# Mixer output to first gate products of a decoder layer: an order by hand, last steps by tiles, and 114-row transfers split into 112 and 2

## The chip, the cores and the metric

The kernel runs on one core of a Trainium2 chip. The metric is the device time of one execution in microseconds (us). The profile is one execution of the same program, recorded by the hardware profiler. Engines are called PE (matmul; PEld is its weight load), DVE (vector), ACT (activation), POOL (GpSimd) and SP (the engine that issues most transfers). A name such as L1017 is a line of the kernel.

## The reference

One decoder layer on 1024 tokens with 16 learned meta tokens ahead of them, width 1024, float32 throughout. A mixer gives `z`; the change lies between `z` and the gate matmul of the feed-forward part. Cut to that:

```python
def rmsnorm(x, gain):
    y = x * lax.rsqrt(jnp.mean(x * x, axis=-1, keepdims=True) + EPS)
    return y * gain
...
        h = h + rmsnorm(z @ w_out[l], mix_norm_post[l])
        u = rmsnorm(h, ffn_norm_pre[l])
        gt = causal_dwconv(u @ ffn_w_gate[l], ffn_conv_w[l], ffn_conv_b[l])
        y = (jax.nn.gelu(gt, approximate=True) * (u @ ffn_w_up[l])) @ ffn_w_down[l]
        h = h + rmsnorm(y, ffn_norm_post[l])
```

## The kernel before

**Numbers.** Every float32 operand is cut into a high part (a cast by ACT) and a low part (operand minus high part, by DVE or POOL). A product is three matmuls, high x high, high x low, low x high (`mm3`, L158 to L162). A weight block `wraw` is loaded by SP, ACT casts it to `whi` (L136, in the gate part L209), and POOL or DVE subtracts to get `wlo` (L137, L210). There are three buffers of `whi` and `wlo`, and the loader keeps three blocks ahead.

**The output projection.** The tokens are cut into three chunks (`c`) of 342, and each chunk into three tiles of 114 rows (RT). For a chunk, `mix_mm` runs over eight k steps; a step multiplies one 128-row block of `z` with one block of `w_out`, for three tiles and two halves of 512 columns: 18 matmuls, named `pm`. Each tile's sum lies in a pair of PSUM banks. There are four pairs; three of them hold the chunk, and the fourth is for transposes (`pt`). The blocks of `z` come from `split_z` (casts and subtractions `zc`, L938 and L939). The last two blocks of weights of chunk 2 have their low part from DVE, all others from POOL.

**Behind a chunk.** For each tile `mix_out` squares the sums on ACT (L1085, result to `ssq2`) and multiplies them by the gain on DVE (L1086, to `m`), each in two halves of 512 columns; after that the pair of banks is empty. `vec` adds the two sums of squares (L1093), takes the reciprocal root, adds the residual row (L1095), stores the new `h` to DRAM as `hscr` (L1096) and normalises again for the feed-forward part: square on ACT (L340), and a multiply by root and gain on DVE in two halves (L345), to `un`. `feat` transposes `un` with eight PE transposes (L1017) and cuts the result into quarters: `v1` (b11, b21) for the first half of the tokens, and for the second half t1 to t4 and b22, which are sums and differences with the first half (L1020 to L1042). The pieces of a chunk are run between the k steps of the next one, by the list that `reorder` gives; those of chunk 2 between the first gate products.

**The gate products.** The gate and up matmuls use one level of Strassen's scheme (`Strassen`): each unit of 128 columns pairs has seven products P1 to P7 (line names `P`, L262 to L265), and each product has 24 matmuls of 258 or 256 columns or 12 of 512. P1 and P2 need only the first half of the tokens (b11, b21). So the first four units run P1 and P2 early: P1(0), P1(1), P2(0), P2(1), P1(2), P1(3), P2(2), P2(3), in the code from `ffn.begin()` on (L1264). Then comes `finish`, which begins with the P6 of unit 0 and reads t2. `ahead(n)` casts the weights of the next n products; `load_first` loads the weights of the early units, `load_unit` those of a whole unit, with sums on POOL (L235 to L238). The result of P1 is copied to SBUF by ACT, the result of P2 is added to it by DVE (`g`, L1191).

**What sets the order.** A scheduler at build time puts the instructions of each engine in an order of its own, from the program, except in `finish`, where POOL's order is that of the code. Each engine then runs its row in order, and an instruction that waits holds all those behind it on that engine.

Of the kernel before, what the change touches and what calls it, by code (L numbers as in the profile page):

```python
# [14 lines left out]
P = 128  # L15
D = 1024
# [40 lines left out]
def trunk_kernel(ctx: ExitStack, tc: tile.TileContext, x, meta_tokens, mix_norm_pre,  # L57
# [122 lines left out]
    class Strassen:  # L180
# [7 lines left out]
        def __init__(self, units, run, early, quarters, span, put, whole):  # L188
# [8 lines left out]
            self.got, self.at = [], 0  # L197
# [50 lines left out]
        def product(self, u, p):  # L248
# [8 lines left out]
            for k in range(4):  # L257
# [6 lines left out]
                for c, o, w in cuts:  # L264
                    pe.matmul(x[:, o : o + w], wlo[:, k, :], xh[:, c : c + w], start=False, stop=(k == 3))  # L265
            self.ahead(4)
            return x[:, o0 : o0 + n]
# [14 lines left out]
        def first(self, u):  # L282
# [3 lines left out]
            return (lambda: act.copy(self.p1s[u], self.product(u, "P1")),  # L286
                    lambda: self.put(u, 0, 0, self.p1s[u], self.product(u, "P2")))
# [711 lines left out]

    def load_res(t0):  # L1000
        row = slot(D, name="row2")
        if t0 == 0:
            nc.sync.dma_start(row[:HALO], meta_tokens[T0:NM, :])
            nc.sync.dma_start(row[HALO:RT], x[0, 0 : RT - HALO, :])
        else:
            nc.sync.dma_start(row[:RT], x[0, t0 - HALO : t0 - HALO + RT, :])
# [48 lines left out]
    def mix_mm(c, between, zs):  # L1055
        rows.update({c * CW + i * RT: load_res(c * CW + i * RT) for i in range(3)})
        banks = [pair_banks("pm") for _ in range(3)]
        znext = []
        for k in range(KD):
            whi, wlo = wo.next()  # L1060
            if k == KD - 1 and c < 2:
                znext = [split_z(c + 1, k_) for k_ in range(ZA)]
            zh, zl = zs[k]
            for i in range(3):
                t = slice(i * RT, (i + 1) * RT)
                for j in range(2):
                    n = slice(j * 512, (j + 1) * 512)
                    mm3(banks[i][j][:RT], (zh[:, t], zl[:, t]), (whi[:, 0, n], wlo[:, 0, n]), k == 0, k == KD - 1)
            wo.ahead()
            if k + ZA < KD:  # L1070
                zs.append(split_z(c, k + ZA))
            if between:
                for f in between.pop(0):
                    f()
        return banks, znext

    def mix_out(c, banks, g2, g3):
        todo = []
        for i in range(3):
            m1 = slot(D, name="m1")  # L1080
            ssq = small([P, 2], "ssq2", "mq", 6)
            for j in range(2):
                n = slice(j * 512, (j + 1) * 512)
                junk = t_tmp(512, "junk")
# [344 lines left out]
```

## Time and profile before

| | us |
|---|---|
| median of 3 runs | 1434.69 |
| lowest and highest | 1431.66, 1434.87 |
| the profiled execution | 1431.93 |
| its span, first to last instruction | 1430.1 |

The mean granted clock of PE in the profiled execution was 0.979 of full speed. The difference of 1.8 us between the execution's time and the span lies around the recorded instructions. How long a group of instructions takes is read from its mean duration; whether it matters is read from who waits for it. A pause of PE and the stretch at a lower granted clock that follows it are read together.

### The profile page before, as it was taken

The numbers are of one execution on the slowest core, as the hardware profiler recorded it, in microseconds if no ns is written. First come the engines' busy times: TensorE is split into PE (matmuls) and PEld (weight loads), VectorE is DVE, ScalarE is ACT, GpSimd is POOL, SyncE is SP. The second block draws the span as 40 slices with busy tenths as digits, with TensorE's granted clock in tenths as the row PEclk, the third lists the DMA queues.
The fourth block names the chain that finished last, engine by engine and source line by source line (L and its number), as shares of the span: only waits on it lengthen the run. The fifth ranks groups of instructions, "written<-read, shape, count | busy, mean of one in ns | idle before, by whom it ended". The sixth has DMA issues, their size and how long they took to land. (4 is left out here: it accounts for less than half of the span.)

```text
span 1430.1 us, 21631 instructions
## 1 busy us (share of the span) xinstructions
PE 1364.1 (95%) x8405; PEld 1233.2 (86%) x8405; DVE 976.1 (68%) x1406; ACT 570.1 (40%) x981; POOL 570.3 (40%) x400
## 2 busy tenths in 40 slices
PE   8989999999999999998968999999999999999976
PEld 6789999999999899976658888888899998888765
DVE  6784545489876754625678888888888775445476
ACT  6443333366654452244464322322222233333353
POOL 4255421237354410253348565544556642001051
PEclk9999999999999999999988999999999999999998
DMA  6034333321110033644542577666677798565546
GB/s 240 36 97 141 126 111 104 97 60 45 33 47 5 23 133 103 218 139 153 166 126 80 142 232 206 186 174 158 162 166 165 169 259 232 194 194 180 191 158 218
DMA packets 129562, 202.65 MB, mean 142 GB/s; under 512 B 7739, under 2 KB 75935, under 8 KB 129460
## 3 DMA queue, kind: packets, MB, share of 16 engines
q1 hardware_dynamic: 118548, 181.08, 37.9%
q0 software_dynamic: 10912, 20.19, 9.4%
q8 instruction: 66, 1.08, 0.3%
q14 instruction: 36, 0.29, 0.1%
HBM read 152.45 MB, written 71.85 MB: 157 GB/s over the span
## 5 line engine op out<-in xcount | busy, mean ns | idle before, releaser
L137 POOL TENSOR_TENSOR wlo<-wraw,whi 128x1024 fp32r<-128x1024 f32 (+2 forms) x37 | 85.3, 2311 | 228.2 <-ACT whi L136 146.5
L262 PE MATMUL P<-v,whi 128*128 128x258 f32 (+2 forms) x528 | 165.8, 328 | 10.9 <-DVE m L1086 4.3
L263 PE MATMUL P<-v,whi 128*128 128x258 f32 (+2 forms) x528 | 164.8, 325 | 0.7 <-POOL v L327 0.7
L265 PE MATMUL P<-v,wlo 128*128 128x258 f32 (+2 forms) x528 | 143.0, 325 | 0.0
L161 PE MATMUL pd<-rot 128*128 128x512 f32 x284 | 111.9, 394 | 8.6 <-DVE rot L1249 8.6
L262 PEld LDWEIGHTS P<-v,whi 128*128 128x128 f32 x528 | 103.1, 195 | 19.1 <-DVE m L1086 4.5
L136 ACT CAST whi<-wraw 128x1024 fp32r<-128x1024 f32 (+2 forms) x60 | 52.9, 884 | 158.6 <-PE pba L174 26.7
L162 PE MATMUL pd<-rot 128*128 128x512 f32 x284 | 111.3, 392 | 0.0
L263 PEld LDWEIGHTS P<-v,whi 128*128 128x128 f32 x528 | 103.1, 195 | 8.8 <-POOL v L327 1.0
L1249 DVE TENSOR_TENSOR rot<-yt,rot 128x1024 fp32r<-128x1024 f32 (+1 forms) x38 | 46.8, 1231 | 90.1 <-ACT rot L1248 90.1
L209 ACT CAST whi<-wraw 128x512 fp32r<-128x512 f32 x90 | 53.2, 617 | 109.6 <-PE P L263 94.4
L265 PEld LDWEIGHTS P<-v,wlo 128*128 128x128 f32 x528 | 90.0, 194 | 7.8
L1133 POOL TENSOR_TENSOR ys<-y 128x512 f32<-128x512 f32 x22 | 34.3, 1559 | 142.0 <-issue 99.4
L210 DVE TENSOR_TENSOR wlo<-wraw,whi 128x512 fp32r<-128x512 f32 x82 | 73.7, 921 | 18.2 <-ACT whi L209 18.2
L235 POOL TENSOR_TENSOR swa<-wraw,wraw 128x512 f32<-128x512 f32 x30 | 47.4, 1582 | 95.5 <-DMA wraw<-in_w_in_dram 62.3
L1248 ACT CAST rot<-yt 128x1024 fp32r<-128x1024 f32 (+1 forms) x38 | 37.7, 995 | 118.7 <-PE pd L161 118.7
L160 PE MATMUL pd<-rot 128*128 128x512 f32 x284 | 75.8, 390 | 1.2 <-ACT rot L1248 1.2
L161 PEld LDWEIGHTS pd<-rot 128*128 128x128 f32 x284 | 53.8, 190 | 21.5 <-DVE rot L1249 10.3
L209 ACT CAST whi<-swa 128x512 fp32r<-128x512 f32 x60 | 35.8, 618 | 87.8 <-PE P L263 74.9
L1183 DVE SCALAR_TENSOR_TENSOR y<-g,par,y 128x1024 f32<-128x1024 f32 x44 | 64.1, 1457 | 0.7
L160 PEld LDWEIGHTS pd<-rot 128*128 128x128 f32 x284 | 53.2, 188 | 12.7 <-ACT rot L1248 1.6
L162 PEld LDWEIGHTS pd<-rot 128*128 128x128 f32 x284 | 53.8, 190 | 11.2
(347 smaller groups left out, 4306.9 us busy)
## 6 DMA issues: line engine op xcount, KB each, us to landing
wraw<-in_w_in_dram SPq DMA_DIRECT2D x36, 512.0 KB, 3.5
yt<-ysum SPq DMA_DIRECT2D x33, 512.0 KB, 3.6
wraw<-in_ffn_w_gate_dram SPq DMA_DIRECT2D x26, 512.0 KB, 8.3
wraw<-in_w_out_dram SPq DMA_DIRECT2D x24, 512.0 KB, 8.7
wraw<-in_ffn_w_up_dram SPq DMA_DIRECT2D x22, 512.0 KB, 4.7
wsum<-in_ffn_w_down_dram SPq DMA_DIRECT2D x22, 512.0 KB, 5.9
ysum<-ys SPq DMA_DIRECT2D x11, 768.0 KB, 4.6
sa<-sscr SPq DMA_DIRECT2D x16, 513.0 KB, 5.2
```

Of the source, the lines that this page charges most:

```text
L136: act.copy(hi, raw)
L137: eng.tensor_tensor(lo, raw, rr(hi), ALU.subtract)
L160: pe.matmul(ps, ahi, bhi, start=first, stop=False)
L161: pe.matmul(ps, ahi, blo, start=False, stop=False)
L162: pe.matmul(ps, alo, bhi, start=False, stop=last)
L209: act.copy(hi, src)
L210: (pool_e if 4 <= i < 2 * self.early else dve).tensor_tensor(lo, src, rr(hi), ALU.subtract)
L235: pool_e.tensor_tensor(s1, a21, a22, ALU.add)
L262: pe.matmul(x[:, o : o + w], whi[:, k, :], xh[:, c : c + w], start=(k == 0), stop=False)
L263: pe.matmul(x[:, o : o + w], whi[:, k, :], xl[:, c : c + w], start=False, stop=False)
L265: pe.matmul(x[:, o : o + w], wlo[:, k, :], xh[:, c : c + w], start=False, stop=(k == 3))
L1183: dve.scalar_tensor_tensor(a, g[:, :, j : j + n], cvw[:, j, m : m + 1], a, ALU.mult, ALU.add)
```

## The change

Five things are done.

1. The driver is rewritten: `mix_mm`, `mix_out`, `reorder` and `ffn.begin()` go, and a class `Rows` with the steps `take` (square and multiply), `add` (residual and store), `norm` and `feat` takes their place. The stage from the first k step to the early gate products stands under a manual order for PE, ACT, DVE and POOL: the rows of these four engines are in the order of the code. SP's row is still the scheduler's.
2. In chunk 2 the last three k steps run tile by tile: tile 0 with k = 5, 6, 7, then tile 1, then tile 2, with a `take` behind each.
3. Square, multiply and the multiply of `norm` work on 1024 columns at once; the nine adds of the two sums of squares (L1093) go.
4. `by_rows`: the loads of residual rows and the stores of `h`, 114 rows each, become transfers of 112 and of 2 rows.
5. `product` takes a function `then` for its result, which is run ahead of the casts of later weights; for the first eight products a list `prompt` sets how many products' weights are cast by then. The load of the first whole unit stands ahead of the transposes of chunk 2.

```diff
-    def mix_mm(c, between, zs):
...
-    def mix_out(c, banks, g2, g3):
...
+    def by_rows(move):
+
+        for r in (slice(0, RT - HALO), slice(RT - HALO, RT)):
+            move(r)
...
+        def take(self, i):
+            m1, ssq = slot(D, name="m1"), small([P, 1], "ssq2", "mq", 6)
+            junk = t_tmp(D, "junk")
+            act.activation(junk[:RT], self.x[i][:RT], AF.Square, accum_out=ssq[:RT])
+            dve.tensor_tensor(m1[:RT], self.x[i][:RT], g2[:RT], ALU.mult)
...
+        def add(self, i):
+            m1, t0 = self.m[i], self.t0[i]
+            rstd = row_rstd(self.ssq[i], RT, "m")
+            dve.scalar_tensor_tensor(m1[:RT], m1[:RT], rstd[:RT], rows.pop(t0)[:RT], ALU.mult, ALU.add)
+            by_rows(lambda r: nc.sync.dma_start(hs[t0 + r.start : t0 + r.stop, :], m1[r]))
+
+        def norm(self, i):
+            m1, ssq, un = self.m[i], small([P, 1], "ssq", "nq"), slot(D, name="un")
+            act.activation(un[:RT], m1[:RT], AF.Square, accum_out=ssq[:RT])
+            rstd = row_rstd(ssq, RT, "n")
+            dve.scalar_tensor_tensor(un[:RT], m1[:RT], rstd[:RT], g3[:RT], ALU.mult, ALU.mult)
...
+    with tc.manual_schedule(engines={E.PE, E.Activation, E.DVE, E.Pool}):
+        for c in range(3):
+            tiles_ = [pair("pm") for _ in range(3)]
+            own = Rows(c, tiles_)
+            for k in range(KD if c < 2 else KD - 3):
+                w = wo.next()
+                for i in range(3):
+                    mix_tile(c, k, w, tiles_[i], i)
+                if k == KD - 1:
+                    for i in range(3):
+                        own.take(i)
+                wo.ahead()
+                next_z(1)
+                if k == 0 and c > 0:
+                    load_rows(c)
+                if last:
+                    if k < 2:
+                        last.norm(k + 1)
+                    if k in (2, 3, 4):
+                        if c == 2 and k == 3:
+                            add_quarters("t2", "t3", "t4")
+                        t4s.append(last.feat(k - 2))
+                    if k > 4 and t4s:
+                        t4s.pop(0)()
+            if c < 2:
+                own.add(0)
+                own.add(1)
+                own.norm(0)
+                own.add(2)
+                last = own
...
+        ws = [wo.next() for _ in range(3)]
+        for i in range(3):
+            for k in range(KD - 3, KD):
+                mix_tile(2, k, ws[k - KD + 3], tiles_[i], i)
+            own.take(i)
+            if i == 0:
+                own.add(0)
+                t4s.pop(0)
+                t4s.pop(0)()
+            if i == 1:
+                ffn.ahead(2)
+                own.norm(0)
+                own.add(1)
+        ffn.ahead(4)
+        ffn.load_first(3)
+
+        ffn.prompt = [5, 6, 8, 8, 8, 10, 10, 11]
+        p = [ffn.first(e) for e in range(EARLY)]
         p[0][0]()
+        own.norm(1)
+        own.add(2)
         p[1][0]()
-        t4s.append((f0 if e == 0 else f2)())
+        own.norm(2)
         p[0][1]()
...
+        ffn.load_unit(RUN[0])
+        t4s.append(own.feat(0))
         p[1][1]()
+        t4s.append(own.feat(1))
+        p[2][0]()
+        p[3][0]()
+        t4s.append(own.feat(2))
+        p[2][1]()
+        p[3][1]()
```

The rows of PE ahead of this stage are the same in both kernels, and so are those behind the early products, apart from numbers in names. Three places show the moves.

First DVE's row in chunk 1, where the tiles of chunk 0 are normalised and transposed. `zc` is a block of z, `v1` takes a transposed tile from its PSUM pair `pt`. Before:

```order
L1095 SCALAR_TENSOR_TENSOR m1_850_6383<-m1_850_6383,rstd_895_6559,row2_802_6146 114x1024
L345 SCALAR_TENSOR_TENSOR un_870_6436<-m1_838_6367,rstd_872_6440,g3_790_6121 114x512 x2
L939 TENSOR_TENSOR zc_887_6512<-sa_774_6010,zc_887_6512 128x342
L939 TENSOR_TENSOR zc_892_6552<-sa_778_6055,zc_892_6552 128x342
L334 RECIPROCAL rstd_883_6484<-std_882_6482 114x1
L345 SCALAR_TENSOR_TENSOR un_881_6480<-m1_844_6375,rstd_883_6484,g3_790_6121 114x512 x2
L939 TENSOR_TENSOR zc_911_6670<-sa_721_5610,zc_911_6670 128x342
L334 RECIPROCAL rstd_899_6568<-std_898_6566 114x1
L327 TENSOR_TENSOR v1_787_6117<-pt_888_6515,v1_787_6117 128x4x114
L345 SCALAR_TENSOR_TENSOR un_897_6564<-m1_850_6383,rstd_899_6568,g3_790_6121 114x512 x2
```

And in the changed kernel:

```order
L1106 SCALAR_TENSOR_TENSOR un_855_6423<-m1_834_6384,rstd_857_6427,g3_790_6121 114x1024
L341 RECIPROCAL rstd_859_6432<-std_858_6430 114x1
L1099 SCALAR_TENSOR_TENSOR m1_842_6394<-m1_842_6394,rstd_859_6432,row2_802_6169 114x1024
L946 TENSOR_TENSOR zc_866_6464<-sa_763_5914,zc_866_6464 128x342
L341 RECIPROCAL rstd_873_6481<-std_872_6479 114x1
L1106 SCALAR_TENSOR_TENSOR un_871_6477<-m1_838_6389,rstd_873_6481,g3_790_6121 114x1024
L946 TENSOR_TENSOR zc_877_6508<-sa_770_5965,zc_877_6508 128x342
L341 RECIPROCAL rstd_881_6516<-std_880_6514 114x1
L1106 SCALAR_TENSOR_TENSOR un_879_6512<-m1_842_6394,rstd_881_6516,g3_790_6121 114x1024
L946 TENSOR_TENSOR zc_885_6543<-sa_774_6010,zc_885_6543 128x342
L334 TENSOR_TENSOR v1_787_6117<-pt_886_6546,v1_787_6117 128x4x114 x2
```

The first tile's `v1` stood ahead of the third `un`; now both its halves stand behind it. The first `un` stood behind the third add and now stands ahead of it.

Then DVE's row around the end of chunk 2. `pm` is the PSUM sum of a tile, `wlo` a low part of gate weights. Before, beginning behind the multiplies of the first tile:

```order
L1086 TENSOR_TENSOR m1_1011_7105<-pm_940_6737,g2_789_6119 114x512
L334 RECIPROCAL rstd_1033_7145<-std_1032_7143 114x1
L1095 SCALAR_TENSOR_TENSOR m1_1005_7097<-m1_1005_7097,rstd_1033_7145,row2_936_6730 114x1024
L1086 TENSOR_TENSOR m1_1011_7105<-pm_940_6737,g2_789_6119 114x512
L1093 TENSOR_TENSOR mss_1038_7158<-ssq2_1012_7106 114x1
L1086 TENSOR_TENSOR m1_1017_7113<-pm_941_6738,g2_789_6119 114x512
L334 RECIPROCAL rstd_1040_7162<-std_1039_7160 114x1
L1095 SCALAR_TENSOR_TENSOR m1_1011_7105<-m1_1011_7105,rstd_1040_7162,row2_937_6732 114x1024
L1086 TENSOR_TENSOR m1_1017_7113<-pm_941_6738,g2_789_6119 114x512
L1093 TENSOR_TENSOR mss_1045_7175<-ssq2_1018_7114 114x1
L334 RECIPROCAL rstd_1037_7154<-std_1036_7152 114x1
L334 RECIPROCAL rstd_1047_7179<-std_1046_7177 114x1
```

In the changed kernel:

```order
L1092 TENSOR_TENSOR m1_990_7039<-pm_931_6764,g2_789_6119 114x1024
L341 RECIPROCAL rstd_995_7046<-std_994_7044 114x1
L1099 SCALAR_TENSOR_TENSOR m1_990_7039<-m1_990_7039,rstd_995_7046,row2_938_6794 114x1024
L1092 TENSOR_TENSOR m1_996_7073<-pm_932_6765,g2_789_6119 114x1024
L210 TENSOR_TENSOR wlo_1001_7079<-wraw_987_7015,whi_1000_7078 128x512
L210 TENSOR_TENSOR wlo_1001_7079<-wraw_988_7017,whi_1000_7078 128x512
L341 RECIPROCAL rstd_1005_7089<-std_1004_7087 114x1
L1106 SCALAR_TENSOR_TENSOR un_1003_7085<-m1_990_7039,rstd_1005_7089,g3_790_6121 114x1024
L341 RECIPROCAL rstd_1007_7094<-std_1006_7092 114x1
L1099 SCALAR_TENSOR_TENSOR m1_996_7073<-m1_996_7073,rstd_1007_7094,row2_939_6797 114x1024
L1092 TENSOR_TENSOR m1_1008_7117<-pm_933_6766,g2_789_6119 114x1024
L210 TENSOR_TENSOR wlo_1013_7123<-wraw_987_7015,whi_1012_7122 128x512
```

The norm of tile 0 (`un`) stood behind the multiplies of all three tiles and now stands ahead of the multiply of tile 2; the low parts of the gate weights, which stood among the combines of chunk 1, now stand between these steps.

Last, ACT's row at the early products in the changed kernel. `p1` is the copy of a P1, `wraw_1014` is the load of the fourth early unit's weights, issued by SP behind the second store of chunk 2, and `tt` takes the transposed tile 0.

```order
L293 COPY p1_1015_7130<-P1_1017_7132 128x514
L209 CAST whi_1018_7158<-wraw_989_7019 128x512
L1104 ACTIVATE un_1021_7163,ssq_1020_7162<-m1_996_7073 114x1024
L339 ACTIVATE std_1022_7165<-ssq_1020_7162,eps_t_75 114x1
L339 ACTIVATE std_1024_7170<-ssq2_1009_7118,eps_t_75 114x1
L293 COPY p1_1015_7130<-P1_1026_7177 128x514
L209 CAST whi_1018_7158<-wraw_1014_7128 128x512
L1104 ACTIVATE un_1028_7206,ssq_1027_7205<-m1_1008_7117 114x1024
L339 ACTIVATE std_1029_7208<-ssq_1027_7205,eps_t_75 114x1
L209 CAST whi_1033_7240<-wraw_989_7019 128x512
L209 CAST whi_1033_7240<-wraw_1014_7128 128x512
L1044 COPY tt_1042_1043_7266<-pt_1039_7256 128x456
```

The cast of `wraw_1014` stands ahead of the square of tile 2 and of the copies of the first transposes, all of which wait for it.

More of the change, by code (lines that the diff above doesn't have):

```diff
@@ L1105, in trunk_kernel @@
[L1105 to L1119 removed]
+    rows, z_at = {}, {}
```

112 lines of the change are left out of this document (40 added, 72 removed).

## The prediction

> **What bounds the kernel.** The page comes first: which engine fills the span, and where in the span it does not.
>
> ```profile
> PE 1364.1 (95%) x8405; PEld 1233.2 (86%) x8405; DVE 976.1 (68%) x1406; ACT 570.1 (40%) x981; POOL 570.3 (40%) x400
> PE   8989999999999999998968999999999999999976
> PEclk9999999999999999999988999999999999999998
> ```
>
> PE is busy for 95% of the span, so a change pays only where PE stands still or runs at a low granted clock. The dent in both digit rows lies in slices 17 to 22, about 600 to 790 us, and that is the stage that the change rewrites. The next view is a table by stretches of time; its columns are the busy time of each engine (with its instruction count), the granted clock, the DMA share and GB/s. The stretches are chunk 0, chunk 1 and chunk 2 of the output projection, the first eight gate products, the next products, and the steady part behind them.
>
> ```profile
> 605.50:639.00 33.50, 33.50 (x147) 25.54 (x146) 9.97 (x13) 12.17 (x20) 19.20 (x8) 1.00 0.44 149
> 639.00:685.00 46.00, 39.87 (x171) 29.99 (x170) 26.17 (x39) 23.55 (x49) 19.88 (x8) 0.93 0.48 155
> 685.00:728.00 43.00, 38.72 (x167) 28.97 (x166) 31.50 (x47) 20.55 (x47) 13.24 (x6) 0.92 0.47 149
> 728.00:769.00 41.00, 31.11 (x222) 30.54 (x221) 35.71 (x57) 24.42 (x63) 26.49 (x19) 0.83 0.38 125
> 769.00:797.00 28.00, 19.89 (x114) 17.95 (x113) 23.76 (x24) 9.50 (x20) 26.44 (x23) 0.82 0.26 57
> 797.00:830.00 33.00, 33.00 (x213) 29.95 (x212) 27.91 (x35) 9.57 (x15) 15.92 (x13) 1.00 0.69 197
> ```
>
> Chunk 0 and the last stretch lose nothing: PE is busy throughout at clock 1.00. In chunk 0 a matmul passes every 33.50/147 = 0.228 us, so a k step of 18 takes 4.1 us. For the others I count as lost the idle time plus (1 - clock) times the length: chunk 1 loses 6.1 + 3.2 = 9.3 us, chunk 2 4.3 + 3.4 = 7.7, the first gate products 9.9 + 7.0 = 16.9, the next 8.1 + 5.0 = 13.1. Together that is 47 us, the most that any rewriting of this stage could return. The waits (total, times, longest, in us) say what ended each pause.
>
> ```profile
> PE pt L1017 <- DVE un L345: 10.8, 4, 5.6
> PE P L262 <- DVE m L1086: 4.3, 1, 4.3
> PE P L262 <- DVE g L1191: 4.1, 1, 4.1
> PE pt L1017 <- DVE v L327: 2.9, 1, 2.9
> PE P L262 <- DVE g L1193: 2.4, 1, 2.4
> ACT zc L938 <- DMA hscr<-m: 9.5, 1, 9.5
> ACT whi L136 <- DMA wraw<-in_w_out_dram: 12.8, 5, 8.3
> ```
>
> PE waits for DVE nearly every time: for a normalised tile `un` that it is to transpose, or for a PSUM pair that DVE has still to empty (`m`, `g`, `v`).
>
> **Tile by tile at the end.** The edit keeps all 54 matmuls of chunk 2's last three k steps. Tile 0 is now complete 2 x 18 x 0.228 = 8.2 us ahead of the first gate product and tile 1 4.1 us ahead, where all three ended within one k step. Two pauses lie just behind that place (start, duration, idle before).
>
> ```profile
> 735.68 0.58 PE L262 MATMUL P<-v,whi 128*128 128x258 f32 x1 [4.33 <-DVE m L1086]
> 746.75 0.99 PE L1017 MATMUL pt<-ident,un 114*128 114x114 f32 x4 [5.56 <-DVE un L345]
> 747.42 0.56 PE L262 MATMUL P<-v,whi 128*128 128x258 f32 x1
> ...
> 735.00:742.00 7.00, 5.52 (x24) 5.22 (x24) 4.61 (x9) 2.78 (x9) 4.46 (x4) 0.52 0.16 45
> 745.00:752.00 7.00, 5.25 (x26) 5.28 (x27) 5.33 (x11) 3.21 (x10) 1.05 (x2) 0.51 0.62 196
> ```
>
> The second gate product waited for tile 0's multiply, and the first transposes for tile 0's norm. Each pause was followed by about 7 us at half clock, worth (1 - 0.52) x 7 = 3.4 us more. The 16.9 us of this stretch is these two pauses with their clock: 9.9 + 6.8 = 16.7.
>
> To see what is late next I lay the new DVE order along PE's time, 0 being the start of the first gate product. I use the mean durations of this stage.
>
> ```profile
> L137 POOL TENSOR_TENSOR wlo<-wraw,whi 128x1024 fp32r<-128x1024 f32 x20 | 49.6, 2493 | 51.1 <-ACT whi L136 51.1
> L345 DVE SCALAR_TENSOR_TENSOR un<-m,rstd,g 114x512 f32<-114x512 f32 x18 | 23.1, 1325 | 0.1
> L136 ACT CAST whi<-wraw 128x1024 fp32r<-128x1024 f32 x22 | 23.0, 1047 | 31.4 <-PE pm L162 18.3 <-DMA wraw<-in_w_out_dram 12.8
> L1095 DVE SCALAR_TENSOR_TENSOR m<-m,rstd,row 114x1024 f32<-114x1024 f32 x9 | 14.1, 1562 | 0.2
> L1086 DVE TENSOR_TENSOR m<-pm,g 114x512 f32<-114x512 f32 x18 | 12.2, 684 | 23.0 <-ACT junk L1085 23.0
> L340 ACT ACTIVATE un<-m 114x1024 f32<-114x1024 f32 x9 | 9.5, 1055 | 5.9 <-DVE un L345 3.3 <-DVE m L1095 2.7
> L210 DVE TENSOR_TENSOR wlo<-wraw,whi 128x512 fp32r<-128x512 f32 x11 | 8.9, 829 | 0.0
> L1047 DVE TENSOR_TENSOR tt<-tt,v 128x456 f32<-128x456 f32 x8 | 7.4, 920 | 0.3 <-ACT tt L1032 0.3
> L327 DVE TENSOR_TENSOR v<-pt,v 128x456 fp32r<-128x456 f32 x8 | 5.0, 628 | 11.8 <-ACT v L326 11.8
> ```
>
> A 1024-wide op is not in the trace. For the multiply and `un` I take two 512-wide ones (1.37 and 2.65 us); the bounds are one and two such ops. Tile 1's multiply ends at -4.1 + 1.4 = -2.7, two weight casts at -1.1, `un` of tile 0 at 1.5. A gate product is 24 matmuls of 258 columns, 24 x 0.228 x 258/512 = 2.8 us; the first transposes come after three, at 8.3, so the 5.56 us pause goes. The pairs of tiles 0 and 1 are empty before the second and third products ask, so the 4.33 goes too. Then: tile 2's multiply to 2.9, two casts to 4.5, `un` of tile 1 to 7.2 (wanted at about 11.8), the add to 8.7. `un` of tile 2 is behind the ACT square, and that stands on ACT behind a gate weight whose load was issued late: about 10.5 to 13. The evacuation of the third product (0.7) is queued on DVE behind this `un`, and the fifth product (due 12.5) waits for it until 13.7: **1.2 us**. The evacuation of the fourth product stands behind the whole combine of tile 0 (three ops of about 1 us, six of 0.6 to 1.0: 7.8 us), so to 22.2. The third transposes, due at 13.7 + 2 x 2.8 = 19.3, wait for its pair: **2.9 us**. The t2 quarter of the last tile stands behind another such chain, two weight casts and five of its own ops: 22.2 + 7.8 + 1.6 + 4.5 = 36, and PE has come to the product that reads it at about 31: **5 us**. For the later products I keep **3 us** of the 8.1 idle that stand there now. In all 12.1 us of waits and, with two half-clock stretches, 6.8 us of clock: 18.9 lost, where 16.9 + 13.1 = 30.0 were. **This term is -11.1 us.** Its bounds: only the last 3 us are left (-27), or the late pauses all stay and those taken away return elsewhere (0).
>
> **By hand in chunks 1 and 2.** A transpose needs the one PSUM pair that the matmuls leave free, and the next tile's transposes wait until DVE has taken the low part `v` from it. In the fixed order that op stands behind all three norms, and these share the time with POOL's weight subtractions (start and duration).
>
> ```profile
> 649.41 5.66 DVE L345 SCALAR_TENSOR_TENSOR un<-m,rstd,g 114x512 f32<-114x512 f32 x2
> ...
> 648.96 5.56 POOL L137 TENSOR_TENSOR wlo<-wraw,whi 128x1024 fp32r<-128x1024 f32 x2 [6.26 <-ACT whi L136]
> ...
> 656.70 0.75 DVE L345 SCALAR_TENSOR_TENSOR un<-m,rstd,g 114x512 f32<-114x512 f32 x1
> 657.60 2.44 DVE L939 TENSOR_TENSOR zc<-sa,zc 128x342 fp32r<-128x342 f32 x1 [0.16 <-ACT zc L938]
> ```
>
> `un` takes 0.75 us alone and 2.83 beside POOL. In chunk 1 PE comes to the second transposes at 639 + 4 x 4.1 + 0.7 = 656.1 (eight transposes by the rows at 746.75 and 747.42, four in 0.67 us at half clock). DVE: multiplies done by 640.4; first add to 643.8 (ACT's square, cast and std are ahead of it), second to 645.4, square and std of the norm to 646.7, `un` to 649.4, third add to 651. Then ACT's cast, square and std and a POOL subtraction lie ahead of each `un`: by means the two norms, two `zc` and two `v` end at about 660, which is a stall of 4 us; if every one of them waits out a whole POOL subtraction it is 665, 9 us; if none does there is no stall. I take the middle of 4 and 9, **6.5 us**, since ACT gives its casts late here and POOL's subtractions bunch, as in the two rows at 649. With 2.5 us of clock that is 9.0 against 9.3 lost now. Chunk 2, with the combines behind the transposes, goes the same way, about a microsecond better: 5.6 + 2.5 = 8.1 against 7.7. **Together 0**, between -17 and +6.
>
> The Trainium skill ("SBUF — State Buffer", "Who interferes with whom") states that DVE and GpSimd share a port pair which is held for a whole instruction while the other blocks, and that issue order decides who blocks. The trace agrees (2.83 against 0.75). By that rule one 1024-wide `un` is blocked once where two halves were blocked twice; rival A is what this would make of the time.
>
> **112 and 2 rows.** Before, eight loads and nine stores of 456 KB had 114 rows.
>
> ```profile
> wraw<-in_w_out_dram SPq DMA_DIRECT2D x6, 512.0 KB, 20.3
> hscr<-m SPq DMA_DIRECT2D x3, 456.0 KB
> row<-in_x_dram SPq DMA_DIRECT2D x3, 456.0 KB
> ...
> 668.02 0.86 ACT L938 CAST zc<-sa 128x342 fp32r<-128x342 f32 x2 [9.46 <-DMA hscr<-m]
> ```
>
> Between 640 and 680 a weight took 20.3 us to land behind them, and ACT stood 9.46 us for the load; the 2.9 us pause of PE on `v` came out of that, and goes. The order puts 17 more issues on SP; nothing on PE waits for SP here. It is in the terms above: without it chunk 1 would keep its 2.9 us and its clock, +4.6. The Trainium skill ("DMA: Bandwidth & Descriptors", "Why a DMA increments its semaphore by 16 and not by 1") states that a transfer is spread over the largest number up to 16 that divides its row counts: 6 for 114, 16 for 112. The DMA share of 0.47 to 0.48 in the middle chunks at 150 GB/s does not speak against it. By that rule the 20.3 us could not come back, and rival B would have hardly any chance and the sum be the same; no run so far shows these loads in 112 rows, so B keeps its chance below.
>
> **Removed work.** Nine adds of sums and nine halves of squares and multiplies go, at most 9 x 0.7 us on DVE, beside PE matmuls. Nothing on the path; if PE's pauses were DVE's total work, it would be up to -2.
>
> **Sum.** The profiled execution took 1431.93 us, 2.8 us under the median of the runs. 1431.9 - 11.1 + 0 = **1421 us**.
>
> **Rivals.** A, *the wide ops win*: DVE is ahead of POOL, the stalls in chunks 1 and 2 fall to about 1.5 us with one 1.7 us of clock: 17.0 becomes 6.4, so -10.6 more, **1410**. For it: `un` at 656.70 took 0.75. Against: at 649.41 both were caught.
> B, *the late gate weight*: the ACT cast that waits for the eighth half of the gate weights has the square of tile 2, the next casts and the copies of the first transposes behind it. Its load is issued at about +2 to +4, and I gave it 6.5. If it lands as the `w_out` rows did (20.3 us), ACT is free 14 to 16 us later; less the slack, the fifth product and all feature work behind it move by 13 us and PE takes another 3.4 of clock: -11.1 + 16.4 = +5.3, **1437**. It loses to before from a landing near 15 us on. Against: the 114-row traffic is what made that 20.3.
> C, *the change does not do what it says*: the order fixed by hand hands its pauses on (t2 of the last tile, `g` behind the combine), and the tail loses 27 rather than 19: **1429**.
>
> **Chances.** Forecast 0.5 (1416 to 1426), A 0.2 (1403 to 1415), C 0.17 (1426 to 1433), B 0.13 (1433 to 1442). About 0.3% (4 us) is what a measurement can tell from no change. Faster: 0.5 + 0.2 + a fifth of C = 0.73; same: most of C and a little of B = 0.16; slower 0.11. Range: 1404 to 1436 leaves out the far ends of A and B.
>
> **What would show it.** The forecast is right if the pauses before the second gate product and the first transposes are gone, if chunks 1 and 2 each have one PE wait of 5 to 7 us for DVE `v`, and if waits for `g` and t2 come 12 to 30 us after the first gate product. A shows as chunks 1 and 2 of about 39 us each. B shows as an ACT wait of over 10 us for a gate weight. It is wrong altogether if PE waits for `zc` or for weights in chunks 1 and 2, which I cost at nothing.

## The result, and the profile after

The changed kernel takes 1422.83 us (median of 4 runs, 1420.99 to 1423.43), the kernel before 1434.78 us (4 runs) beside it: a ratio of 0.992, 95% interval 0.9903 to 0.9937. The forecast of 1421 us was close. The experiments show that it was so by errors that cancelled: the edit that was booked with the least, the split of the transfers, brings more than the whole gain, and the fixed order takes part of it back.

The stretches of the changed kernel's profile, with the same columns and the same cuts as before the change:

```profile
605.50:639.00 33.50, 33.50 (x152) 26.21 (x151) 20.77 (x11) 10.76 (x15) 17.40 (x9) 1.00 0.51 165
639.00:685.00 46.00, 40.55 (x181) 31.26 (x180) 36.38 (x30) 25.67 (x46) 22.60 (x9) 0.93 0.47 160
685.00:728.00 43.00, 37.58 (x166) 28.89 (x165) 38.48 (x49) 24.97 (x56) 17.13 (x12) 0.92 0.48 151
728.00:769.00 41.00, 31.66 (x232) 30.57 (x231) 36.71 (x46) 20.99 (x49) 19.72 (x15) 0.87 0.38 124
769.00:797.00 28.00, 25.36 (x155) 22.84 (x154) 26.44 (x25) 12.33 (x24) 25.00 (x22) 0.93 0.32 74
```

PE still stands idle for 5.4 us in each of chunks 1 and 2 and for 9.3 us among the first gate products; only in the row from 769 us on is the idle time much smaller (2.6 us instead of 8.1). The waits of PE in the changed kernel, from 600 to 850 us:

```profile
PE pt L1029 <- DVE v L334: 10.9, 2, 5.5
...
PE pt L1029 <- DVE g L1183: 6.2, 1, 6.2
...
PE P L262 <- DVE g L1183: 3.4, 3, 2.0
...
PE P L262 <- ACT t2h L333: 2.4, 1, 2.4
```

These are the four kinds of wait that the prediction named. Behind the first gate product (729.00 us) they come at 14 us (0.75 us, for `g`), at 26 us (6.2, for `g`) and at 38.6 us (2.4, for t2); the last is later than the 12 to 30 us that the prediction gave as the sign. Waits for `un` and for the multiply `m` are gone, and so is the ACT wait for `hscr`. ACT's waits for `w_out`, 12.8 us before, are down to 0.2 us.

For comparisons I take the stage by itself, since the executions differ by up to 3.5 us in the 606 us ahead of it, where all kernels have the same PE rows. It begins with the first matmul of the projection and ends at one fixed matmul of the steady part, the same in all kernels; the first gate product cuts it into the chunks and the tail. Some 150 matmuls between the early products and that end are not in one order in all kernels, nor before and after the change. It is said above that the rows of PE behind the early products are the same; they are so only behind these. In the changed kernel (start, duration):

```profile
608.44 0.39 PE L160 MATMUL pm<-whi,zc 128*114 128x512 f32 x1
...
729.00 0.28 PE L262 MATMUL P<-v,whi 128*128 128x258 f32 x1
...
806.40 0.39 PE L263 MATMUL P<-t4l,whi 128*128 128x512 f32 x1
```

That is 120.6 us for the chunks and 77.4 for the tail. Read in the same way for every kernel of this study:

| kernel | order of the stage | rows of a transfer | last three k steps | chunks, us | tail, us | stage, us | median of its runs, us |
|---|---|---|---|---|---|---|---|
| before | scheduler | 114 | by steps | 122.8 | 86.1 | 208.8 | 1432.9 to 1434.8 |
| the change | by hand | 112 + 2 | by tiles | 120.6 | 77.4 | 198.0 | 1422.8 |
| e1_rows114 | by hand | 114 | by tiles | 142.7 | 79.0 | 221.7 | 1447.1 |
| e2_split_only | scheduler | 112 + 2 | by steps | 108.7 | 81.9 | 190.5 | 1417.0 |
| h1_57_57 | by hand | 57 + 57 | by tiles | 175.0 | 82.6 | 257.6 | 1481.1 |
| e3_by_steps | by hand | 112 + 2 | by steps | 122.0 | 80.3 | 202.3 | 1426.6 |
| e4_halves | by hand | 112 + 2 | by tiles | 121.0 | 77.8 | 198.8 | 1422.4 |
| f1_norms_behind | by hand, moved | 112 + 2 | by tiles | 119.2 | 77.3 | 196.5 | 1421.3 |
| f1c_feats_later | by hand, moved | 112 + 2 | by tiles | 120.3 | 77.5 | 197.9 | 1423.6 |
| f3_g_first | by hand, moved | 112 + 2 | by tiles | 120.5 | 77.9 | 198.4 | 1421.9 |
| f4_sums_late | by hand, moved | 112 + 2 | by tiles | 120.7 | 76.7 | 197.4 | 1421.5 |
| g1_tail_only | by hand in the tail alone | 112 + 2 | by tiles | 107.7 | 84.1 | 191.8 | 1415.1 |
| g2_no_hand | scheduler, new code | 112 + 2 | by tiles | 106.2 | 79.0 | 185.2 | 1411.8 |
| g3_no_hand_steps | scheduler, new code | 112 + 2 | by steps | 106.2 | 78.4 | 184.6 | 1408.0 |

The stages come from one profile each; the medians from 4 to 6 runs of the experiment.

### The profile page after: what moved, and what is told of

It reads as the page before. It is cut to its first block, busy times and chain, and to the rows that moved or that the text cites. A ratio compares the mean times of both kernels' runs of the same rounds, so it can differ in the third digit from the quotient of the medians.

```text
span 1421.7 us, 21615 instructions
## 1 busy us (share of the span) xinstructions
PE 1360.1 (96%) x8405; PEld 1231.2 (87%) x8405; DVE 1001.3 (70%) x1379; ACT 569.7 (40%) x963; POOL 561.1 (39%) x400
## 5 line engine op out<-in xcount | busy, mean ns | idle before, releaser
L262 PE MATMUL P<-v,whi 128*128 128x258 f32 (+2 forms) x528 | 163.7, 324 | 2.8 <-DVE g L1183 2.8
L263 PE MATMUL P<-v,whi 128*128 128x258 f32 (+2 forms) x528 | 162.7, 322 | 0.0
L262 PEld LDWEIGHTS P<-v,whi 128*128 128x128 f32 x528 | 101.2, 192 | 10.8 <-DVE g L1183 3.2
L263 PEld LDWEIGHTS P<-v,whi 128*128 128x128 f32 x528 | 101.4, 192 | 7.4
L161 PEld LDWEIGHTS pd<-rot 128*128 128x128 f32 x284 | 53.8, 190 | 21.5 <-DVE rot L1241 10.3
L160 PEld LDWEIGHTS pd<-rot 128*128 128x128 f32 x284 | 53.6, 189 | 12.8 <-ACT rot L1240 1.6
```

The lines of the kernel that those rows point to most:

```text
L160: pe.matmul(ps, ahi, bhi, start=first, stop=False)
L161: pe.matmul(ps, ahi, blo, start=False, stop=False)
L262: pe.matmul(x[:, o : o + w], whi[:, k, :], xh[:, c : c + w], start=(k == 0), stop=False)
L263: pe.matmul(x[:, o : o + w], whi[:, k, :], xl[:, c : c + w], start=False, stop=False)
```

## Experiments: what the split is worth

The first undoes the split in the changed kernel.

```diff
-        for r in (slice(0, RT - HALO), slice(RT - HALO, RT)):
-            move(r)
+        move(slice(0, RT))
```

> The changed kernel with the loads and stores of 114 rows whole again; all else stays. Theory (the split was worth what the prediction gave it): the ACT wait for the block of z behind these transfers comes back in chunk 1 (about 9 us), the second weight and low parts come late, chunk 1 is 3 to 6 us longer than 46 us, 1426 to 1429 us. Rival (the split lies off the path, DVE's order and POOL set the stall of chunk 1 anyway): PE's wait for v stays 5.5 us, 1422 to 1424 us.

It took 1447.05 us, ratio to before 1.010 (1.0086 to 1.0113): slower than the kernel before. Both expectations are far off; the split is worth 24 us in this order, and the waits that came back are mainly for the weights; on `hscr`, where the expectation looked, ACT waits 2.0 us. The waits from 640 to 745 us in that kernel:

```profile
ACT whi L136 <- DMA wraw<-in_w_out_dram: 23.7, 3, 11.6
...
PE pt L1028 <- DVE v L334: 19.4, 3, 8.4
...
PE pt L1028 <- ACT tt L1044: 8.2, 1, 8.2
```

and ACT's row in chunk 1 (start, duration, idle before):

```profile
673.92 1.04 ACT L136 CAST whi<-wraw 128x1024 fp32r<-128x1024 f32 x1 [10.64 <-DMA wraw<-in_w_out_dram]
674.87 0.47 ACT L945 CAST zc<-sa 128x342 fp32r<-128x342 f32 x1
675.25 0.53 ACT L333 CAST v<-pt 128x456 fp32r<-128x456 f32 x1
```

ACT waits 10.64 us for a late weight block, and the cast that would empty the transposes' PSUM pair (`v<-pt`) stands two places behind it. So a late transfer becomes a PE stall of 8.4 us, though no wait of PE in this kernel is for a weight of the projection. In the kernel before, ACT waited about as long (9.46 us at 668.02), but PE had only 2.9 us of it.

The other corner is the kernel before with the split as its only edit.

```diff
-            nc.sync.dma_start(row[:RT], x[0, t0 - HALO : t0 - HALO + RT, :])
+            for r in (slice(0, RT - HALO), slice(RT - HALO, RT)):
+                nc.sync.dma_start(row[r], x[0, t0 - HALO + r.start : t0 - HALO + r.stop, :])
...
-                nc.sync.dma_start(hs[t0 : t0 + RT, :], m1[:RT])
+                for r in (slice(0, RT - HALO), slice(RT - HALO, RT)):
+                    nc.sync.dma_start(hs[t0 + r.start : t0 + r.stop, :], m1[r])
```

> The kernel before with its loads and stores of 114 rows split into 112 and 2, nothing else; the scheduler orders the stage anew. Theory (the split relieves ACT and the weights, in either order): the ACT waits for hscr and w_out go, chunks 1 and 2 are 3 to 6 us shorter, 1428 to 1431 us. Rival (the scheduler had placed work around the late transfers, so that only the fixed order needs the split): within 2 us of before.

1416.98 us, ratio 0.9888 (0.9871 to 0.9905): 16 us faster than before where 3 to 6 were expected, and 6 us faster than the whole change. The intervals of these two ratios just touch, but three variants of the change by hand that were timed together with this kernel (f1_norms_behind, f1c_feats_later and f4_sums_late below) took 1421.3 to 1423.6 us. The split alone shortens the chunks by 14.1 us and the tail by 4.2. The scheduler orders the stage anew in this kernel (the rows of ACT, DVE and PE in the chunks differ), so a part may come from that. The stretches of chunks 1 and 2 in it:

```profile
639.00:685.00 46.00, 43.96 (x204) 33.47 (x203) 33.39 (x46) 28.70 (x61) 26.29 (x10) 1.00 0.58 185
685.00:728.00 43.00, 38.70 (x196) 31.09 (x195) 38.98 (x58) 25.07 (x61) 18.11 (x13) 0.96 0.51 158
```

From 639 to 685 us the clock is 1.00 throughout, and 204 matmuls pass where 171 did before.

Whether it is the 112 rows or having two transfers in place of one is told apart by a split into 57 and 57.

```diff
-        for r in (slice(0, RT - HALO), slice(RT - HALO, RT)):
+        for r in (slice(0, RT // 2), slice(RT // 2, RT)):
```

> The changed kernel with the transfers of 114 rows split into 57 and 57 instead of 112 and 2: as many transfers, as many bytes. Theory (it is the 112 rows, which can be dealt out to all 16 DMA engines evenly, that make the transfers fast; a count like 57 goes to few engines): no better than 114 rows whole, 1440 to 1455 us. Rival (two shorter transfers in place of a long one are what helps): 1422 to 1430 us.

1481.07 us, ratio 1.033 (1.0320 to 1.0348): as many transfers and bytes, and 58 us slower than 112 and 2: the theory's direction, but 26 us beyond its range. The DMA rows from 655 to 668 us, mean busy share of the 16 engines (a digit is a tenth) and GB/s in 40 slices, first of this kernel:

```profile
DMA  1121211111111122111111111222111111111221
GB/s 76 76 88 76 88 76 76 76 76 76 76 76 76 76 101 88 76 76 76 76 76 76 76 76 76 88 88 88 76 76 76 76 76 76 76 76 76 101 88 76
DMA packets 266, 1.03 MB, mean 79 GB/s; under 512 B 15, under 2 KB 15, under 8 KB 266
...
q1 hardware_dynamic: 266, 1.03, 19.3%
```

Then of the kernel before, in the same 13 us:

```profile
DMA  9699996498999842399899963344333334333333
GB/s 265 227 353 302 277 202 126 101 265 239 265 252 265 177 88 88 139 290 265 315 328 302 214 151 88 113 176 164 151 151 151 151 151 176 164 151 151 164 164 164
```

And of the changed kernel:

```profile
DMA  9999999999999999999999989998520000000000
GB/s 378 391 416 441 403 378 290 277 252 239 290 265 302 340 403 416 403 403 429 403 429 416 391 353 403 403 391 328 227 88 25 0 0 0 0 0 0 0 0 0
```

With 57 rows the queue runs flat at about 79 GB/s and 19% of 16 engines: as much as 3 engines at 26 GB/s. With 114 the flat end of the row is at 151 to 164 GB/s and three to four tenths: as much as 6 engines at about 26. With 112 the share is nine tenths at 240 to 440 GB/s, and the queue is empty by 665 us. The Trainium skill ("DMA: Bandwidth & Descriptors", "Why a DMA increments its semaphore by 16 and not by 1") states that the number of engines is the largest one up to 16 that divides the row count: 3 for 57, 6 for 114, 16 for 112. The three traces agree with these counts; their rows show shares and rates, not single engines. That 512 KB weights land late behind such transfers is seen in the landing time, 20.3 us before the change in the stretch from 640 to 680 us, and in ACT's waits for `w_out` in three kernels whose rows on PE, ACT, DVE and POOL are in the same fixed order: 0.2 us with 112 and 2 rows, 26.5 with 114, 65.4 with 57 (from 600 us to behind the stage).

## Experiments: what the order and the tiles are worth

Undoing the tile order of chunk 2's end, by hand still:

```diff
-        for i in range(3):
-            for k in range(KD - 3, KD):
+        for k in range(KD - 3, KD):
+            for i in range(3):
                 mix_tile(2, k, ws[k - KD + 3], tiles_[i], i)
-            own.take(i)
+        for i in range(3):
+            own.take(i)
```

> The changed kernel with the last three k steps of chunk 2 done step by step, and the squares and multiplies of all three tiles behind them. Theory (the tile order removed the two pauses of 4.3 and 5.6 us with their clock): pauses of PE for DVE m and un come back behind the first gate product, 6 to 10 us, 1429 to 1433 us. Rival (what sets the end of the early products is DVE's chain of three combines up to t2 of the last tile, about 26 us from the first transposes on, and the tile order only starts it earlier): the pause of 6.2 us for g shrinks by what comes ahead of it, 2 to 4 us in all, 1425 to 1427 us.

1426.63 us, ratio 0.9954 (0.9942 to 0.9966): 3.8 us slower than the change, in the rival's range. The wait for `g` fell from 6.2 to 4.1 us, and 46.2 us behind the first gate product PE has come equally far in both kernels: the late chain took up what the tiles had advanced. Of the 4.3 us that the stage is longer, 1.4 lie in the chunks. The other 2.9 lie behind those 46.2 us, where PE waits 1.4 us for a low part of t4 from POOL, runs 3.4 us at half clock, and has another order from the scheduler; that these are the tiles' worth too is not shown.

The norm's multiply on halves again:

```diff
-            dve.scalar_tensor_tensor(un[:RT], m1[:RT], rstd[:RT], g3[:RT], ALU.mult, ALU.mult)
+            for j in range(2):
+                n = slice(j * 512, (j + 1) * 512)
+                dve.scalar_tensor_tensor(un[:RT, n], m1[:RT, n], rstd[:RT], g3[:RT, n], ALU.mult, ALU.mult)
```

> The changed kernel with the multiply of norm on 2 x 512 columns, as before; squares and the multiply by the gain stay at 1024. Theory (each op that meets a POOL subtraction is held for the whole of it): the second norm in chunks 1 and 2 is caught twice, 2 to 3 us more stall before the second transposes in each, 1426 to 1429 us. Rival (POOL has only its one subtraction per k step, so a second half seldom meets one): the same within 1.5 us.

1422.43 us, ratio 0.9929 (0.9917 to 0.994): the same, as the rival had it. DVE's row of the changed kernel shows why (start, duration):

```profile
650.02 1.28 DVE L1106 SCALAR_TENSOR_TENSOR un<-m,rstd,g 114x1024 f32<-114x1024 f32 x1
651.23 0.16 DVE L341 RECIPROCAL rstd<-std 114x1 f32<-114x1 f32 x1
651.42 3.25 DVE L1099 SCALAR_TENSOR_TENSOR m<-m,rstd,row 114x1024 f32<-114x1024 f32 x1
654.59 2.71 DVE L946 TENSOR_TENSOR zc<-sa,zc 128x342 fp32r<-128x342 f32 x1
657.23 0.15 DVE L341 RECIPROCAL rstd<-std 114x1 f32<-114x1 f32 x1
657.41 3.27 DVE L1106 SCALAR_TENSOR_TENSOR un<-m,rstd,g 114x1024 f32<-114x1024 f32 x1
660.61 0.50 DVE L946 TENSOR_TENSOR zc<-sa,zc 128x342 fp32r<-128x342 f32 x1
```

A wide `un` takes 1.28 us alone and 3.27 beside POOL's subtraction, an add 1.28 and 3.25, a `zc` 0.50 and 2.71. POOL's row beside it:

```profile
650.99 5.94 POOL L137 TENSOR_TENSOR wlo<-wraw,whi 128x1024 fp32r<-128x1024 f32 x2 [4.48 <-ACT whi L136]
657.20 2.41 POOL L137 TENSOR_TENSOR wlo<-wraw,whi 128x1024 fp32r<-128x1024 f32 x1 [0.27 <-ACT whi L136]
```

Each time about 2 us are added, once for each of the three POOL subtractions. In the halves kernel the same pair of ops took 3.40 together: only one subtraction stands beside them. The rule of the Trainium skill that the prediction cited ("SBUF — State Buffer", "Who interferes with whom"), a port pair held for a whole instruction, fits these rows: the `un` at 657.41 ends 1.07 us behind the subtraction that ends at 659.61. That two halves are caught twice, as the prediction took from it, is seen only where two subtractions stand back to back (at 648.96 before the change).

Moving the norms of tiles 1 and 2 behind the first transposes:

```diff
-                    if k < 2:
-                        last.norm(k + 1)
                     if k in (2, 3, 4):
...
                         t4s.append(last.feat(k - 2))
+                    if k == 2:
+                        last.norm(1)
+                        last.norm(2)
```

> The changed kernel with the norms of tiles 1 and 2 moved behind the first transposes (and the low parts taken from them) in chunks 1 and 2. Theory (the 5.5 us stall for v is DVE's row: v stands behind two norms that POOL's subtractions hold): PE's wait before the second transposes goes from 5.5 to 0 to 2 us in each chunk, less clock lost, 3 to 5 us in each: 1413 to 1417 us. Rival (POOL's hold is what counts, whoever stands in the row): the wait turns into one of about 4 to 5 us for un, no gain beyond 1.5 us.

1421.34 us, ratio 0.9919 (0.9905 to 0.9933), with a stage 1.5 us shorter. PE's wait turned from one for `v` into one for `un` (the row names the reciprocal that ends just behind that `un`):

```profile
664.20 0.61 PE L1029 MATMUL pt<-ident,un 114*128 114x114 f32 x2 [5.11 <-DVE rstd L341]
```

That is the rival. Three `zc` beside three POOL subtractions take 5.77 us of DVE here and hold the first `v` until 659.97, and the two norms come behind it. Giving DVE one more k step in chunk 1 instead:

```diff
-                    if k < 2:
-                        last.norm(k + 1)
-                    if k in (2, 3, 4):
+                    ks = (3, 4, 5) if c == 1 else (2, 3, 4)
+                    if k in ks:
...
-                        t4s.append(last.feat(k - 2))
+                        t4s.append(last.feat(k - ks[0]))
+                    if c == 1 and k in (0, 1):
+                        last.norm(k + 1)
+                    if c == 2 and k == 2:
+                        last.norm(1)
+                        last.norm(2)
```

> As f1_norms_behind in chunk 2; in chunk 1 the norms stay where the changed kernel has them, and the three sets of transposes come one k step (4.2 us) later. Theory: v of the first tile is due 4.2 us later while DVE's row ends when it did, so the 5.5 us stall of chunk 1 falls to 0 to 1.5 us, 1413 to 1417 us, chunk 1 as good as or better than in f1_norms_behind. Rival (the low part is taken late because the transposes themselves set it): the stall of chunk 1 stays 5 us.

1423.59 us, ratio 0.9937 (0.9923 to 0.9951): no gain, and the stall of chunk 1 stayed 5.8 us. Here the theory of that stall fell. DVE was through with its norms at 662.2 us, but the cast of the transposes came late on ACT:

```profile
656.72 0.47 ACT L945 CAST zc<-sa 128x342 fp32r<-128x342 f32 x1
663.31 1.04 ACT L136 CAST whi<-wraw 128x1024 fp32r<-128x1024 f32 x1 [6.12 <-PE pm L162]
664.26 0.47 ACT L945 CAST zc<-sa 128x342 fp32r<-128x342 f32 x1
664.64 0.53 ACT L333 CAST v<-pt 128x456 fp32r<-128x456 f32 x1
```

A weight cast stands ahead of it and waits for a buffer that PE is still reading. PE runs 18 matmuls on, then waits for the transposes' pair. So in the fixed order two different rows on two engines can hold the same PSUM pair, and moving one leaves the other. What neither edit touches is the distance in PE's row: one k step, 18 matmuls, between the transposes of one tile and those of the next.

Two edits in the tail follow. In the first, DVE takes the fourth gate product ahead of the combine of tile 0:

```diff
-        t4s.append(own.feat(0))
+        held = pair_banks()
+        transposes(own.un[0], held)
         p[1][1]()
+        t4s.append(to_quarters(own.un[0], own.t0[0], held, True))
```

> The changed kernel with DVE's evacuation of the fourth gate product ahead of the combine of tile 0 (PE's order stays). Theory (DVE's chain sets the end): the PE pause of 6.2 us before the third transposes goes, and comes back as a longer wait of the first P6 for t2 of the last tile (2.4 us now, then 7 to 9): 1421 to 1423.5 us, no gain. Rival (the pause itself is the cost): 6.2 us and 3.4 us of clock are gained, 1413 to 1416 us.

1421.89 us, ratio 0.9929 (0.9916 to 0.9941): no gain. The 6.2 us wait is gone, but it came back at another place than expected: a gate product waits 7.1 us for ACT's copy of a P1 (`PE P` behind `ACT p L293`), and the wait for t2 went from 2.4 to 1.4 us. In the second, POOL's sums come after the first transposes' work:

```diff
-        ffn.load_unit(RUN[0])
         t4s.append(own.feat(0))
+        ffn.load_unit(RUN[0])
         p[1][1]()
```

> The changed kernel with POOL's four sums of the first whole unit behind the work of the first transposes instead of ahead of it. Theory (DVE's combine of tile 0 took 11.5 us because the sums ran beside it, and the 6.2 us wait for g comes from that): the combine of tile 0 takes 6 to 8 us, the wait for g falls to 1 to 3 us; but the sums now stand beside the next combine, so the wait for t2 or for the weights of P6 grows, 1419 to 1423 us in all. Rival (the amount of DVE work sets the wait, POOL hardly matters): the combine and the wait stay as long, 1422 to 1425 us.

1421.47 us, ratio 0.9919 (0.9906 to 0.9933); the tail is 0.7 us shorter, and the time lies within the spread of the runs of the change. DVE's combine of tile 0 went from 11.6 us to 8.2 us and the wait for `g` from 6.2 to 3.0, and 2.8 us appeared at ACT's copy of a P1. The theory holds in kind: POOL beside DVE lengthens the chain, and shortening one place of it fills the next.

Last, the fixed order is taken away: in g1_tail_only the `manual_schedule` line moves from the chunk loop to just ahead of `ffn.load_first(0)`, in g2_no_hand it goes.

```diff
-    with tc.manual_schedule(engines={E.PE, E.Activation, E.DVE, E.Pool}):
+    if True:
         for c in range(3):
```

> The changed kernel with the manual order for its last part alone (from the last three k steps of chunk 2 on); the k steps ahead of it are the scheduler's to order, from the same code. Theory (with the split, the scheduler's order loses about 4 us in chunks 1 and 2 where the fixed one loses 16, and the tail by tiles is 4 us shorter than the scheduler's): from the first step of chunk 0 to the first gate product 109 to 112 us instead of 120.6, 1411 to 1416 us in all, at or below the kernel with the split alone (1417). Rival (the scheduler's good order of chunks 1 and 2 came from the old code, with the norms of the old order and halves of 512): chunks 1 and 2 as long as now, 1420 to 1424 us.

> The changed kernel with no manual order from the first k step to the early products: split, wide operations, last steps by tiles and the new code order stay, the scheduler orders all engines. Theory (the fixed order costs in chunks 1 and 2 and gains in the tail): chunks 1 and 2 as in g1_tail_only, the tail 0 to 5 us longer than there, 1412 to 1419 us. Rival (the new code order is what costs, not that it is fixed): 1421 to 1425 us.

g1_tail_only: 1415.07 us, ratio 0.9878 (0.9865 to 0.9892). Its chunks are 12.9 us shorter than the change's, a little more than expected, but its tail is 6.7 us longer. Of that, 5.1 us are lost in the first two gate products, where PE waits 2.3 us for a low part of their weights and runs 6.8 us at half clock. g2_no_hand: 1411.79 us, ratio 0.985 (0.9837 to 0.9864), faster than both kernels; its tail is 5 us shorter than that of g1_tail_only where 0 to 5 us longer was expected. So a tail fixed by hand fits the chunks it was made for, and did not gain behind another order.

PE's own row shows where the chunks' 12.9 us lie. In the changed kernel the transposes of the first two tiles in chunk 1 have 18 matmuls between them:

```profile
654.28 0.94 PE L1029 MATMUL pt<-ident,un 114*128 114x114 f32 x8
664.86 1.75 PE L1029 MATMUL pt<-ident,un 114*128 114x114 f32 x8 [5.46 <-DVE v L334]
```

In g1_tail_only the scheduler has put 37 between them:

```profile
651.50 0.94 PE L1029 MATMUL pt<-ident,un 114*128 114x114 f32 x8
661.76 0.97 PE L1029 MATMUL pt<-ident,un 114*128 114x114 f32 x8 [0.79 <-DVE v L334]
```

The second set begins 10.6 and 10.3 us behind the first: the PSUM pair comes free about as late in both, but meanwhile PE has two k steps of work in g1_tail_only and one in the changed kernel. Chunk 2 is alike (18 matmuls and 34). In f1_norms_behind and f1c_feats_later, with 18 again, the second set of chunk 1 begins 10.2 and 10.9 us behind the first. So the likely cost of the fixed order is this distance; no run changes it alone, so that is not shown.

> As g2_no_hand, with the last three k steps of chunk 2 step by step and the squares and multiplies of the three tiles behind them: what is left of the change is the split, the wide operations and the new code order, all ordered by the scheduler. Theory (the tile order is worth about 4 us, as in e3_by_steps, and not the 15 us that the prediction booked for it): 1414 to 1417.5 us, close to the kernel before with the split alone (1417). Rival (without the fixed order the scheduler brings the tiles' work forward by itself): within 1.5 us of g2_no_hand, 1410.5 to 1413 us.

The edit is that of e3_by_steps on g2_no_hand. 1407.95 us, ratio 0.9831 (0.9818 to 0.9845), the fastest version found, and neither expectation had it that fast. Their intervals overlap, they were not timed beside each other, and their stages in the profiles are 184.6 and 185.2 us; what can be said is that without the fixed order the tiles are worth nothing that shows. The stretches of chunks 1 and 2 of g3_no_hand_steps:

```profile
639.00:685.00 46.00, 45.23 (x210) 34.78 (x209) 34.56 (x43) 30.88 (x60) 22.27 (x9) 1.00 0.62 201
685.00:728.00 43.00, 39.24 (x219) 32.67 (x219) 38.27 (x49) 25.38 (x59) 23.38 (x17) 0.96 0.53 164
```

PE idles 0.8 us in the first; the second already holds 16 us of gate products.

## Why the prediction was right in its sum, and where it was wrong

**112 and 2 rows: mis-sized, the step that failed.** The prediction booked this edit "in the terms above", with 4.6 us if it were not there. Measured, it is worth 24 us in the fixed order (e1_rows114) and 16 us in the scheduler's (e2_split_only). It priced the one PE pause (2.9 us) behind a 9.46 us ACT wait; it showed ACT's 12.8 us of waits for `w_out` and gave them no price. In e1_rows114 such a wait of 10.64 us costs PE 8.4, because the cast that empties the transposes' pair stands behind it on ACT. The price depends on the order in which the wait stands. In the scheduler's order the 16 us hold a new order as well, so there they are not shown to be the transfers' alone.

**By hand in chunks 1 and 2: right in the waits, wrong in what they were compared with.** The stalls for `v` were forecast at 6.5 and 5.6 us and measured at 5.46 and 5.42; the term was 0 and the chunks came out 2.2 us shorter. The prediction's way of counting, idle time plus half clock, gives 17.5 us lost where it forecast 17.1 and had 17.0 before. It counts a piece twice: the half clock of chunk 1 begins at 662.4 us, inside the pause that ends at 664.86. It matters more that with the split the scheduler's order loses much less there: the same code without the manual order in the chunks takes 107.7 us (g1_tail_only) against 120.6 in the change. The fixed order costs 12.9 us in the chunks, which no term of the prediction had, because it weighed the order against a before that still had the slow transfers. The reason given for the stalls, DVE's row beside POOL, is half of it: the rows are as described, but f1_norms_behind and f1c_feats_later show that the stall outlives the removal of that cause. The other half is likely the distance of one k step between the sets of transposes, which the prediction took as given when it set PE's arrival at 656.1.

**Tile by tile at the end: direction right, size wrong.** The term was -11.1 us for the tail. The tail became 8.7 us shorter. Of that e2_split_only has 4.2 without any tile order; the tile order itself is worth at most 4 us in the fixed order (e3_by_steps) and nothing that shows without it (g2_no_hand against g3_no_hand_steps). The two pauses of 4.33 and 5.56 us did go, as forecast; what comes late next was the chain on DVE. Its waits were 0.8 instead of 1.2 us, 6.2 instead of 2.9, 2.4 instead of 5 for t2, and 2.6 in two pieces instead of 3 behind that: 12.0 where 12.1 was expected. That this sum agrees is luck, with the wait for `g` 3.3 us above its forecast and the one for t2 2.6 below. The half clock came to 17.0 us in three stretches, 8.5 us lost, where 6.8 was booked. The combine of tile 0 took 11.6 us, not 7.8, mostly because POOL's sums ran beside it (8.2 us without them in f4_sums_late).

**Rivals.** A (wide ops ahead of POOL): did not come; a wide or a halved `un` makes no difference (e4_halves). B (the late gate weight): ACT waited 3.3 us for that DMA, and no wait of PE ends on it. Its premise, slow landings, is what the split removes, and e1_rows114 is the slower-than-before case, with another transfer: the weights of the projection. C (pauses handed on): this happened to the edits of f1, f3 and f4, not to the whole.

**Sum.** The stage became 10.9 us shorter, where 11.1 were forecast. That is luck: -8.7 in the tail and -2.2 in the chunks stand for -11.1 and 0. By edits it is made of about -18 for the split with the scheduler's order and +7 for all the rest, the fixed order foremost (190.5 to 198.0 us).

What stays open: how much of the gap between e2_split_only (190.5 us) and g3_no_hand_steps (184.6 us) comes from the wide operations, and how much from the new code order; and whether transposes two k steps apart, with ACT's and DVE's rows to match, would make the fixed order as good as the scheduler's.

## What to carry to other kernels

Look at the row counts of transfers first: a transfer whose share of the DMA engines is flat at a fraction while others queue behind it is worth splitting into a part whose row count has 16 as a factor (here 112) and a rest. Price a slow transfer by what stands behind its waiter on the same engine, in the order that will run, not in the order of the trace at hand. When an order is fixed by hand, ask of each engine's row how much work lies between two users of one buffer, PE's row included. And before an order is fixed, measure the other edits without it: here the split alone (1417.0 us) beat the whole change (1422.8), and the change without its fixed order (1411.8) beat the split alone.

## What the runs showed of the hardware that was not expected

Counted as 3 and 6 engines, the rate per DMA engine in these transfers is the same, about 26 GB/s (79 and about 158 GB/s), so the loss is in proportion to the engines left out.

The executions differ by up to 3.5 us ahead of the stage (its first matmul at 605.56 to 609.08 us), with the same PE rows; a difference of 3 us between single profiles therefore means nothing unless the stage itself is compared.
